# A two-level fast matrix product on one Trainium2 core: whole products in three places of the end groups, fewer range sums, and new hand-made orders at both ends

## The chip, the cores and the metric

The kernel runs on one core of one Trainium2 chip. Its time is the device time of one execution in microseconds (us); the number compared is the median over runs. Before the change it is 1456.9 us (three runs, 1456.58 to 1457.16).

## The reference

```python
B, S, D = 8, 2048, 2048
x = randn(B, S, D).float32;  w = randn(D, D).float32
cs = cumsum(x, axis=1)
diff = cs - concatenate([zeros, cs[:, :-1, :]], axis=1)   # this is x again
return matmul(diff, w).float32
```

The difference of a running sum is x itself, so the kernel computes C = x · w for 16384 rows, with inner and outer size 2048.

## The kernel before, in words

**Tiles and groups.** The 16384 rows are 128 tiles of 128 rows. The first four tiles (PLAIN, line 37) are multiplied plainly while the weights are still coming in (lines 178 to 358, matmuls at L264 and L299). The other 124 are done in 31 groups of four tiles (g, h, k, l), which `group` (line 566) writes down; `period[0]` counts the groups from 0 to 30.

**Two levels.** A group is a product of a 2x2 block matrix (rows g,h and k,l; two halves of the inner size) with a 2x2 block matrix of weights, done by the seven-product scheme of Strassen and Winograd: P1 to P7. P6 is done as a whole product, 2 x 16 matmuls (`whole_product`, L543). Each of the other six is itself 2x2 quarters. `Seven` does it with seven quarter products of four 128x512 matmuls each (`quarter`, L450) in place of eight. A group is thus 6 x 28 + 32 = 200 matmuls.

**What a Seven costs beside its matmuls.** `slot` (lines 476 to 505) records, for each product: four sums s1 to s4 of the x quarters on VectorE (128x512 f16); sums of weight quarters Q1, Q3, Q4 (128x2048 f16) that `Right.ask` (line 395) makes in one scratch area, `flow`, just before use, unless they have been made for good; one VectorE sum `middle` of two PSUM banks' contents; three ScalarE copies out of PSUM, `first`, `out2` and `out4`, on which later quarter products into the same bank wait; and one more sum, `last`, mostly on GpSimd. The sums of x between the outer products are S1 to S4 (128x1024 f16), applied in place to the x tiles. `keep` copies and `C..+P..` sums carry results out of PSUM into C tiles and add the products up, on ScalarE, VectorE and GpSimd.

**Weight quarters made for good.** For each right-hand block some sums are made once, by `Right.quarters` and `Right.make` (lines 379 to 394): Q3, Q2 and for some Q4. Q2 is written over t12, so t12 itself is gone from then on. For in_3 (used by P3) and in_7 (used by P7) these are six VectorE operations of 128x2048 f16 in group 0.

**Loads.** An x tile half is loaded by SyncE into one of three stages of F (`load`), cast to f16 by ScalarE (`narrow`), summed in magnitude by ScalarE for a range check (`weigh`; its throw-away output goes to the spare half of the same stage), and turned by a transposing DMA from SyncE's queue (`turn`). A stage is free for the next load only after both.

**The range sums of C.** `see` (line 507) makes ScalarE read a finished C tile (128x1024) and sum its magnitudes, with the throw-away output in the spare half of the stage that was loaded last. Before, all eight C tiles of group 1 are read so. `judge` (line 699) turns all checks into one flag (flag1 to flag9, a small matmul among them); the flag is read by every engine at the end (L1184), and a slow fallback (not taken here) hangs on it.

**The order.** Every operation is recorded with a label, and `emit` (line 104) sorts them by a number: group times 100000 plus the place of its label in the table `places` (line 733). An engine issues its operations in just this order, and waits in it for data. Groups 0, 1, 2, 28, 29 and 30 have a table of their own, all others share one (`None`). Each GpSimd operation also waits for the VectorE operation ahead of it in that order (`in_turn`).

Of the kernel before, what the change touches and what calls it, by code (L numbers as in the profile page):

```python
# [10 lines left out]
def kernel(  # L11
# [6 lines left out]
    nc = tc.nc  # L18
# [30 lines left out]
    const = ctx.enter_context(tc.tile_pool(name="const", bufs=1))  # L49
    Wall = const.tile([P, KH, 4 * NH], f32, name="W")  # L50
# [7 lines left out]
    seen_c = tiny[:, 8:16]  # L58
# [309 lines left out]
    class Right:  # L368
# [58 lines left out]
    in_3.quarters(early[3])  # L427
    in_7.quarters(late[0], late[1])
# [7 lines left out]
    for some, to in zip((in_3, in_5, in_1, in_2), late[3:]):  # L436
        some.make("Q4", "t21", "Q2", SUB, to)

# [23 lines left out]
    class Seven:  # L462
        def __init__(self, name, g, h, side, right, to, room, lent):
# [3 lines left out]
            self.right = right  # L467
            (self.g0, self.g1), (self.h0, self.h1) = to
# [6 lines left out]

        def slot(self, i):
            n = self.name
# [29 lines left out]
    def see(c, i):  # L507
        if period[0] == 1:
# [4 lines left out]
                lambda: nc.scalar.activation(other, c, ABS, accum_out=seen_c[:, i : i + 1]),  # L513
# [52 lines left out]
    def group(g, xy, zv):  # L566
        h, k, l = g + 1, g + 2, g + 3
# [3 lines left out]
        def ready(t, i):  # L571
            nonlocal ready_last
            ready_last = t, i
# [125 lines left out]
    def judge():  # L699
# [4 lines left out]
        dve("flag4", lambda: ins.tensor_scalar(flags[:, 8:16], seen_c, FINITE, None, ALU.is_le))  # L704
        dve("flag5", lambda: ins.tensor_reduce(flags[:, 1:2], flags[:, 8:16], AX.X, ALU.min))
# [36 lines left out]
            'first x.0.0': -710913, 'cast w.0.0': -708588, 'numbers turned': -640017,  # L742
            'eye': -620640, 'first x.0.1': -615478, 'first x.2.3': -611089,
# [517 lines left out]
```

## Time and profile before

| | |
|---|---|
| median of three runs | 1456.9 us |
| the profiled execution, its own time | 1456.21 us |
| its span from first to last instruction | 1454.3 us |
| mean granted TensorE clock | 0.998 |
| matmuls | 6543 |
| busy: TensorE, VectorE, ScalarE, GpSimd | 1424.5, 1302.5, 1046.1, 552.1 us |

In the profile, PE is TensorE (PEld its weight loads), DVE is VectorE, ACT is ScalarE, POOL is GpSimd and SP is SyncE, which issues all DMAs. Lines of the code are L126 (all sums, whatever engine), L129 (all ScalarE copies and casts), L163 (`weigh`), L513 (`see`), L450 and L543 (matmuls). Tiles are named without numbers: b is a PSUM bank, x the turned x tiles, F the stages, W the weights and their sums, arena everything else. Since one line covers many operations, an operation is found by its shape, its tiles and its position in the order.

### The profile page before, as it was taken

To read this page: it belongs to the slowest core of one execution; us is meant where nothing else is said; L and a number is where in the kernel's file an instruction comes from. 1 tells how busy PE (TensorE), PEld (TensorE's weight loads), DVE (VectorE), ACT (ScalarE), POOL (GpSimd) and SP (SyncE) were. 2 spreads that over 40 slices of the span, in tenths; PEclk is the share of its full clock that TensorE was granted. 3 is DMA by queue.
4 is the path that set the end of the run, shared out by engine and by line. 5 is a ranking of instruction groups with operands and counts; after the bars stand their busy time and mean duration, and the time that the engine had idled before them with its cause. 6 is when DMAs were issued, how large, how long until landed. Compare 5 with 4: busy or idle time off the path is not lost. (4 is left out here: it accounts for less than half of the span.)

```text
span 1454.3 us, 20618 instructions
## 1 busy us (share of the span) xinstructions
PE 1424.5 (98%) x6543; PEld 630.1 (43%) x6543; DVE 1302.5 (90%) x2107; ACT 1046.1 (72%) x1716; POOL 552.1 (38%) x376
## 2 busy tenths in 40 slices
PE   8999899999999999999999999999999999999997
PEld 3443334444444444444444444444444444444443
DVE  2799879999999999999999999999999999999997
ACT  5877867777777767777777777777777777776773
POOL 0014423444433444433444433444433444433444
PEclk9999999999999999999999999999999999999999
DMA  9998698888888898788888888898888898888883
GB/s 362 350 259 217 188 231 237 250 249 229 240 243 239 247 249 230 239 241 240 247 250 229 242 236 244 247 254 225 246 238 240 252 253 222 247 239 226 252 223 121
DMA packets 343792, 351.64 MB, mean 242 GB/s; under 512 B 270976, under 2 KB 270976, under 8 KB 343680
## 3 DMA queue, kind: packets, MB, share of 16 engines
q1 hardware_dynamic: 343680, 350.29, 84.3%
q8 instruction: 52, 0.85, 0.2%
q14 instruction: 60, 0.49, 0.1%
HBM read 150.99 MB, written 134.22 MB: 196 GB/s over the span
## 5 line engine op out<-in xcount | busy, mean ns | idle before, releaser
L126 POOL TENSOR_TENSOR arena<-arena 128x512 f32<-128x512 f32 x372 | 551.9, 1491 | 896.8 <-DVE arena L126 623.7
L129 ACT COPY arena<-b 128x512 f32<-128x512 f32 x729 | 407.2, 588 | 257.6 <-PE b L450 127.7
L450 PE MATMUL b<-W,x 128*128 128x512 f16 x2108 | 521.2, 379 | 2.1 <-DVE x L126 1.0
L450 PEld LDWEIGHTS <-x 128*128 128x128 f16 x3224 | 314.5, 98 | 396.4 <-issue 21.9
L126 DVE TENSOR_TENSOR arena<-W 128x2048 f16<-128x2048 f16 (+1 forms) x287 | 367.6, 1281 | 23.5 <-PE b L450 23.4
L450 PE MATMUL b<-W,arena 128*128 128x512 f16 x1364 | 344.0, 379 | 5.8 <-DVE arena L126 3.8
L450 PEld LDWEIGHTS <-arena 128*128 128x128 f16 x1984 | 189.1, 98 | 254.8 <-DVE arena L126 35.9
L129 ACT CAST F<-F 128x1024 f16<-128x1024 f32 x248 | 260.2, 1049 | 44.5 <-DMA F<-in_x_dram 40.6
L450 PE MATMUL b<-arena,x 128*128 128x512 f16 x1116 | 281.6, 379 | 4.4 <-ACT arena L129 4.4
L163 ACT ACTIVATE F<-F 128x1024 f16<-128x1024 f16 x248 | 263.1, 1062 | 1.1
L126 DVE TENSOR_TENSOR arena<-arena,b 128x512 f32<-128x512 f32 x372 | 247.7, 678 | 11.1 <-PE b L450 9.6
L543 PE MATMUL b<-W,x 128*128 128x512 f16 x992 | 250.1, 381 | 1.6 <-DVE x L126 1.6
L126 DVE TENSOR_TENSOR x<-x,x 128x1024 f16<-128x1024 f16 (+1 forms) x372 | 232.8, 633 | 6.2 <-DMA x<-F 3.8
L129 ACT COPY b<-b 128x512 f32<-128x512 f32 x186 | 107.3, 577 | 78.0 <-DVE arena L126 62.0
L450 PE MATMUL b<-arena 128*128 128x512 f16 x620 | 159.1, 379 | 2.3 <-DVE arena L126 2.1
L126 DVE TENSOR_TENSOR b<-b,arena 128x512 f32<-128x512 f32 x217 | 150.1, 692 | 11.4 <-ACT arena L129 11.0
L543 PEld LDWEIGHTS <-x 128*128 128x128 f16 x992 | 95.3, 98 | 122.3 <-DVE x L126 12.0
L126 DVE TENSOR_TENSOR arena<-b,arena 128x512 f32<-128x512 f32 x155 | 105.3, 681 | 18.5 <-PE b L450 17.0
L126 DVE TENSOR_TENSOR arena<-x,x 128x512 f16<-128x512 f16 x124 | 56.8, 458 | 31.9 <-PE b L450 31.7
L126 DVE TENSOR_TENSOR arena<-x 128x512 f16<-128x512 f16 x124 | 59.3, 479 | 1.2 <-PE b L450 0.2
L126 DVE TENSOR_TENSOR x<-x 128x512 f16<-128x512 f16 x124 | 56.6, 457 | 3.3 <-PE b L450 1.5
L126 DVE TENSOR_TENSOR arena<-arena,x 128x512 f16<-128x512 f16 x124 | 54.2, 437 | 2.6
(43 smaller groups left out, 301.4 us busy)
## 6 DMA issues: line engine op xcount, KB each, us to landing
F<-in_x_dram SPq DMA_DIRECT2D x248, 512.0 KB, 5.0
out_dram<-arena SPq DMA_DIRECT2D x240, 512.0 KB, 3.7
W<-in_w_dram SPq DMA_DIRECT2D x32, 512.0 KB, 9.0
out_dram<-arena SPq DMA_DIRECT2D x32, 256.0 KB, 3.4
W<-in_x_dram SPq DMA_DIRECT2D x16, 256.0 KB, 7.0
x<-F SPq DMA_TRANSPOSE x248, 3.2
```

Source lines behind the costliest of these rows:

```text
L126: record(label, engine, lambda: on.tensor_tensor(dst, p, q, op))
L129: record(label, "act", lambda: nc.scalar.copy(to, p))
L163: return nc.scalar.activation(other, data, ABS, accum_out=m)
L450: said = nc.tensor.matmul(to, a[:, ds(k * P, P)], b[:, k, :], start=(start and k == 0), stop=(k == 3), skip_group_check=True,)
L543: said = nc.tensor.matmul(to[n], half(t, 0)[:, k, :], T2[k][:, n, :], start=False, stop=(k == KH - 1), skip_group_check=True,)
```

## The change

Four things are changed.

1. `see` sums three C tiles in place of eight: C21 of rows l in group 29 (`see.3`), and C11 and C12 of rows h in group 30 (`see.1`, `see.5`). In group 1 there is none any more. The small checks read three columns in place of eight.
2. P3 and P7 in group 0, and P7 in group 30, are done as whole products: `slot_whole` records eight quarter products (w0 to w7) with no sums, no copies and no `last`. Each has 32 matmuls in place of 28. In group 30, t12 of in_7 is no longer there, so it is made again as t22 - Q3 in `flow`.
3. The weight sums of in_3 and in_7 (three each) are recorded in group 1 in place of group 0. In the new order the first of them stands early in group 0, three more amid the C12 sums of group 0, and two (in7 Q2 and Q4) in group 1.
4. The tables of places for groups 0, 1, 2, 28, 29 and 30 are new; the shared one is the same.

```diff
+    FROM3, FROM7 = 1, 1
+    LAST = (END - PLAIN) // 4 - 1
...
+                "t12": ("t22", "Q3", SUB),
...
-    in_3.quarters(early[3])
-    in_7.quarters(late[0], late[1])
...
-    for some, to in zip((in_3, in_5, in_1, in_2), late[3:]):
+    for some, to in zip((in_5, in_1, in_2), late[4:]):
...
+    def by_quarters():
+        if period[0] == FROM7:
+            in_7.quarters(late[0], late[1])
+        if period[0] == FROM3:
+            in_3.quarters(early[3])
+            in_3.make("Q4", "t21", "Q2", SUB, late[3])
...
+            self.whole = (name == "P3" and period[0] < FROM3) or (
+                name == "P7" and (period[0] < FROM7 or period[0] == LAST)
+            )
...
+        def slot_whole(self, i):
+            pairs = [
+                (to, a, b, start)
+                for to, p, q, c in (
+                    (self.g0, self.a11, self.a12, 1),
+                    (self.g1, self.a11, self.a12, 2),
+                    (self.h0, self.a21, self.a22, 1),
+                    (self.h1, self.a21, self.a22, 2),
+                )
+                for a, b, start in ((p, f"t1{c}", True), (q, f"t2{c}", False))
+            ]
+            for j in (0, 1) if i == 0 else (i + 1,):
+                to, a, b, start = pairs[j]
+                if b not in self.asked:
+                    self.asked[b] = self.right.ask(b)
+                quarter(f"{self.name}.w{j}", to, a, self.asked[b], start)
...
         def slot(self, i):
+            if self.whole:
+                return self.slot_whole(i)
...
     def see(c, i):
-        if period[0] == 1:
+        rows = {1: LAST, 5: LAST, 3: LAST - 1}
+        if i in rows and period[0] == rows[i]:
...
-                if s == "h" and i == 1:
+                if s == "h" and i == 1 and not P3.whole:
                     plus("P3.last", c[:, i, :], lz, "pool")
...
-                if s == "h" and i == 1:
+                if s == "h" and i == 1 and not P7.whole:
                     plus("P7.last", c[:, i, :], lx, "pool")
```

Parts of the new orders, as the tables give them, one engine each (the number ahead of the stroke is the group):

```
SyncE at the start:     x.0.2, x.0.1, w.0.2, x.0.3, x.0.0, w.0.0, x.1.0, x.1.3, x.1.1, w.0.1
  before:               w.0.1, x.0.3, w.0.0, x.0.0, x.0.1, x.2.3, x.1.1, x.0.2, x.2.2, x.1.0
SyncE, stores of the plain part: put out.0.0.0 is second, before it was sixth
TensorE, around 28/P1.6:  28/P1.6, 28/P2.2, 28/P6g.1.0     (before: 28/P1.6, 28/P6g.0.0)
TensorE, 29 to 30:      29/P4.2, 29/P7.6, 29/P7.5, 29/P4.4, 29/P4.3, 30/P1.0, 29/P4.6, 29/P4.5, 30/P2.0,
                        30/P1.3, 30/P1.2, 30/P1.1, 30/P2.3, 30/P1.4, 30/P1.5, 30/P1.6, 30/P2.2, 30/P2.1, 30/P2.4, 30/P2.5, 30/P5.0
ScalarE, 29 to 30:      30/P1.first, 29/narrow6.1, 29/weigh6.1, 29/see.3, 30/P2.first, 30/keep C11g.0, 30/P1.out2,
                        30/P1.out4, 29/narrow6.0, 30/keep C11g.1, 29/narrow7.1, 30/P2.out2, 29/narrow7.0
ScalarE, 1 to 2:        1/P4.out2, 1/weigh5.1, 1/P7.out4, 1/P4.out4, 1/narrow6.1, 1/weigh6.1, 2/P1.first,
                        1/narrow6.0, 2/P1.out2
TensorE, 1 to 2:        1/P4.2, 1/P4.3, 1/P7.4, 1/P4.4, 1/P7.6, 1/P7.5, 1/P4.6, 1/P4.5, 2/P1.0, 2/P1.1, 2/P1.2
ScalarE, 0 to 1:        0/weigh5.1, 0/weigh4.1, 0/P4.first, 0/P4.out2, 0/narrow6.1, 0/P4.out4, 0/narrow7.1,
                        1/P1.first, 0/narrow6.0, 1/P1.out2
TensorE at the end:     P7.w2, P4.2, P4.3, P4.4, P7.w3, P4.6, P4.5, flag8
VectorE at the end:     C21g+P7.1, vote, P4.s4, C21h+P4.0, C21g+P4.1, flag9
GpSimd at the end:      C22h+C21.0, C22h+C21.1, C22g+C21.0, P4.last, C22g+C21.1
  before:               C22h+C21.1, C22h+C21.0, C22g+C21.1, P4.last, ahead of them P7.last
```

More of the change, by code (lines that the diff above doesn't have):

```diff
@@ L57 @@
     seen_w = tiny[:, 0:1]
-    seen_c = tiny[:, 8:16]
+    seen_c = tiny[:, 8:11]
     flags = tiny[:, 16:32]
@@ L467, in __init__ @@
             self.right = right
+            self.whole = (name == "P3" and period[0] < FROM3) or (
+                name == "P7" and (period[0] < FROM7 or period[0] == LAST)
+            )
+            self.asked = {}
             (self.g0, self.g1), (self.h0, self.h1) = to
@@ L512, in see @@
                 "act",
-                lambda: nc.scalar.activation(other, c, ABS, accum_out=seen_c[:, i : i + 1]),
+                lambda: nc.scalar.activation(other, c, ABS, accum_out=seen_c[:, i // 2 : i // 2 + 1]),
             )
@@ L566, in group @@
     def group(g, xy, zv):
+        by_quarters()
         h, k, l = g + 1, g + 2, g + 3
@@ L572, in ready @@
             nonlocal ready_last
-            ready_last = t, i
+            if t < END:
+                ready_last = t, i
             load(t, i)
@@ L703, in judge @@
         dve("flag3", lambda: ins.tensor_reduce(flags[:, 0:1], fits, AX.XY, ALU.min))
[L704 to L705 removed]
+        dve("flag4", lambda: ins.tensor_scalar(flags[:, 8:11], seen_c, FINITE, None, ALU.is_le))
+        dve("flag5", lambda: ins.tensor_reduce(flags[:, 1:2], flags[:, 8:11], AX.X, ALU.min))
         dve(
@@ L734 @@
         0: {
[7 rows of a table removed]
-            'first x.0.0': -710913, 'cast w.0.0': -708588, 'numbers turned': -640017,
-            'eye': -620640, 'first x.0.1': -615478, 'first x.2.3': -611089,
[156 rows of a table removed]
-        },
[47 rows of a table removed]
-        },
[46 rows of a table removed]
[6 rows of a table added]
+            'first x.0.2': -1182588, 'ones': -1161467, 'numbers': -1151794,
+            'numbers turned': -1081308, 'first x.0.1': -1061770, 'w.0.2': -1026012,
[151 rows of a table added]
+        },
[48 rows of a table added]
+        },
[45 rows of a table added]
         },
         28: {
[44 rows of a table removed]
[45 rows of a table added]
         },
         29: {
[45 rows of a table removed]
[45 rows of a table added]
         },
         30: {
[43 rows of a table removed]
[42 rows of a table added]
         },
```

766 rows, old and new, of the table places are left out of this document.

## The prediction

> **What bounds the kernel now.** I read the page first, then busy time by stretches of one group's length, then the order of time where TensorE lost time.
>
> ```profile
> span 1454.3 us, 20618 instructions
> PE 1424.5 (98%) x6543; PEld 630.1 (43%) x6543; DVE 1302.5 (90%) x2107; ACT 1046.1 (72%) x1716; POOL 552.1 (38%) x376
> ...
> F<-in_x_dram SPq DMA_DIRECT2D x248, 512.0 KB, 5.0
> ...
> x<-F SPq DMA_TRANSPOSE x248, 3.2
> ```
>
> TensorE is the bound. An average of 98% leaves nothing to see of the ends, so the second view cuts the span; its columns are the length of the stretch, then busy time and count of PE, PEld, DVE, ACT and POOL, then the granted clock.
>
> ```profile
> 0.00:35.00 35.00, 28.53 (x155) 13.28 (x156) 10.00 (x22) 19.81 (x20) 0.20 (x4) 1.00 0.96 360
> ...
> 72.00:76.00 4.00, 2.68 (x13) 1.10 (x12) 4.00 (x6) 2.45 (x6) 0.00 (x0) 1.00 1.15 294
> 76.00:119.60 43.60, 41.82 (x190) 18.18 (x190) 42.13 (x61) 32.85 (x56) 10.48 (x7) 1.00 0.91 249
> 119.60:163.10 43.50, 40.05 (x181) 17.14 (x180) 38.95 (x62) 33.59 (x56) 13.91 (x10) 1.00 0.76 214
> 163.10:206.60 43.50, 38.51 (x166) 16.26 (x165) 35.68 (x56) 30.83 (x53) 12.16 (x9) 0.96 0.79 204
> ...
> 306.00:349.50 43.50, 43.50 (x202) 19.32 (x201) 40.05 (x66) 31.89 (x54) 17.78 (x13) 1.00 0.86 243
> 1305.10:1348.60 43.50, 42.47 (x197) 18.89 (x196) 40.70 (x66) 29.42 (x49) 17.90 (x12) 1.00 0.86 228
> 1360.00:1403.50 43.50, 42.85 (x197) 18.73 (x195) 40.28 (x66) 30.46 (x51) 16.59 (x12) 1.00 0.88 241
> 1403.50:1447.00 43.50, 41.69 (x189) 17.95 (x187) 40.41 (x70) 20.57 (x37) 19.62 (x14) 1.00 0.48 150
> ```
>
> A group in the middle (306 to 349.5) has TensorE busy throughout with VectorE at 40.05 of 43.50. So 200 matmuls take 43.5 us, 0.2175 each and 0.87 for a quarter product, and a VectorE load of 40 does no harm. The middle groups keep their order, so nothing is won there. Lost are 1.3 us at 72, 1.8, 3.5 and 5.0 in groups 0, 1 and 2, 1.0 in group 28, 0.7 and 1.8 in the last two. In group 0 VectorE is nearly full (42.13); in groups 1 and 2 it is not, and there a queue must be blocked. The order of time shows by what:
>
> ```profile
> 175.89 1.06 ACT L513 ACTIVATE F<-arena 128x1024 f16<-128x1024 f32 x1
> 176.86 0.19 ACT L513 ACTIVATION_READ_ACCUMULATOR F<-arena 128x1 f32 x1
> ...
> 183.61 1.04 ACT L129 CAST F<-F 128x1024 f16<-128x1024 f32 x1 [2.90 <-issue]
> ```
> ```profile
> 177.07 0.33 SPq L145 DMA_DIRECT2D F<-in_x_dram  x1
> ```
> ```profile
> 185.94 1.02 PE L450 MATMUL b<-arena,x 128*128 128x512 f16 x4 [2.34 <-ACT arena L129]
> 187.37 3.40 PE L543 MATMUL b<-W,x 128*128 128x512 f16 x8 [0.40 <-DVE x L126]
> ```
>
> The last range sum of group 1 ends at 177.05, and the load of tile 6, half 0, goes out at 177.07: the sum throws its output into the stage which that load fills. Its cast is next in ScalarE's queue and waits until 183.61; the copy P2.out4 behind it is what the quarter product at 185.94 waits for. Then eight matmuls take 3.40 us where 1.74 is the pace: the clock was halved, 1.66 us more. Groups 0 to 2 thus lose 1.8 + 3.5 + 5.0 + 1.7 = 11.9 us.
>
> **The change part by part.** *Whole products.* Twelve more matmuls at 0.2175: 1.7 us in group 0 and 0.9 in group 30, in full, since TensorE is the bound. What goes:
>
> ```profile
> L126 DVE TENSOR_TENSOR arena<-W 128x2048 f16<-128x2048 f16 x283 | 366.0, 1293 | 23.5 <-PE b L450 23.4
> ...
> L126 DVE TENSOR_TENSOR b<-b,arena 128x512 f32<-128x512 f32 x217 | 150.1, 692 | 11.4 <-ACT arena L129 11.0 <-PE b L450 0.3
> ...
> L126 DVE TENSOR_TENSOR arena<-x 128x512 f16<-128x512 f16 x124 | 59.3, 479 | 1.2 <-PE b L450 0.2
> ...
> L126 DVE TENSOR_TENSOR arena<-x,arena 128x512 f16<-128x512 f16 x124 | 53.4, 431 | 3.0 <-PE b L450 3.0
> ```
> ```profile
> L129 ACT COPY arena<-b 128x512 f32<-128x512 f32 x729 | 407.2, 588 | 257.6 <-PE b L450 127.7 <-POOL arena L126 76.7 <-DVE b L126 26.5
> ...
> L129 ACT CAST F<-F 128x1024 f16<-128x1024 f32 x248 | 260.2, 1049 | 44.5 <-DMA F<-in_x_dram 40.6 <-issue 2.9 <-ACT F L163 0.5
> ```
>
> In group 0, VectorE loses eight sums of 0.43 to 0.48 (3.6), two middles of 0.69 (1.4) and two Q1 of 1.29 (2.6), 7.6 us in all, and ScalarE six copies of 0.59, 3.5 us. Four of the six moved weight sums now stand in that stretch, three will. So VectorE falls from 42.13 to about 33.3 there: far under the 40 that does no harm. I keep 0.7 of the 1.8 lost. Group 1 gets two weight sums, 2.6 us: 38.95 becomes 41.5, between the 40.05 that costs nothing and the 42.13 that came with 1.8. I keep 2.0 of its 3.5.
>
> GpSimd works more in group 1 (13.91) than in group 0 (10.48), and VectorE is slower beside it:
>
> ```profile
> 171.88 1.67 DVE L126 TENSOR_TENSOR arena<-W 128x2048 f16<-128x2048 f16 x1
> ...
> 175.82 1.21 DVE L126 TENSOR_TENSOR arena<-W 128x2048 f16<-128x2048 f16 x1
> ```
> ```profile
> 164.73 7.74 POOL L126 TENSOR_TENSOR arena<-arena 128x512 f32<-128x512 f32 x5
> ```
>
> The same sum took 1.67 as GpSimd finished and 1.21 with it quiet. I leave the two at the mean of 1.29; beside GpSimd throughout they cost 0.8 more. The Trainium skill ("GPSIMD Engine Reference", 1. Specifications) says that GpSimd's way to SBUF is shared with VectorE, with contention for VectorE instructions with two SBUF inputs, which these are. By that rule alone the sum below would be 0.8 higher; the trace agrees with the direction.
>
> *Range sums.* Eight of 1.06 + 0.19, 10 us of ScalarE, leave group 1, and with them the hold on the load. Of the 5.0 + 1.7 of group 2 the rows above name 2.3 + 0.4 + 1.7; with the new order I keep 1.3. Groups 0 to 2 keep 0.7 + 2.0 + 1.3 = 4.0 of 11.9: -7.9 (bounds 0 and -11.9), and +1.7 for the matmuls.
>
> *Hand-over at 72 us.*
>
> ```profile
> 74.20 1.30 ACT L129 COPY arena<-b 128x512 f32<-128x512 f32 x2 [1.42 <-DMA out_dram<-arena]
> 75.40 0.59 ACT L129 COPY b<-b 128x512 f32<-128x512 f32 x1
> ```
> ```profile
> 76.05 1.02 PE L450 MATMUL b<-W,arena 128*128 128x512 f16 x4 [1.37 <-ACT b L129]
> ```
>
> The first ScalarE copy waits for a buffer whose store (put out.0.0.0) stood sixth among the stores and is now second; three plain products also stand ahead of P1.2. -1.1 (0 to -1.4).
>
> *Start.* The first turn needs two x pieces. In the old order 1.84 MB are asked for up to the second of them (256 KiB for a piece of x, 512 for one of w), in the new one 1.31 MB; at 360 GB/s (first row of the stretches) that is 1.5 us less. But until 35 us the weights come no faster, and TensorE had 6.5 us idle there. -0.4 (-1.6 to +2).
>
> *Group 28.*
>
> ```profile
> 1320.07 1.90 PE L543 MATMUL b<-W,x 128*128 128x512 f16 x8 [1.03 <-DVE x L126]
> ```
>
> A product that waits for nothing, P2.2 (0.87), now stands ahead of this one: -0.9 (0 to -1.0).
>
> *Groups 29 to 30.* The three range sums are 3.8 us on a ScalarE with room (20.57 of 43.50). But see.3 holds the load of tile 6, half 0, exactly as see.3 of group 1 did. I walk the new order from the start of 29/P4.2. TensorE: 18 quarter products until P2.4, 15.7 us. ScalarE: P1.first ends 0.7 after the sixth product, at 5.9; narrow6.1 (1.05) and weigh6.1 (as long as a range sum of the same shape, 1.06 + 0.19) bring 8.2, see.3 9.4. Load: issued then, 5.0 to land, 14.4 to 14.8. Then narrow6.0 (1.05), keep C11g.1 (0.59), narrow7.1 (1.05) and P2.out2 (0.59): 18.1. P2.4 waits for P2.out2, 2.4 us late in all; I add 0.3 for small waits. The turned tile (1.2 of issue, 3.2 to land) reaches S1g at 20, no later than the products ahead of P5.0. So 2.7 us are lost in place of 2.5 now (0.7 + 1.8), and 0.9 of matmuls come on top: +1.0 (-1.6, if the load lands in time, to +5).
>
> *The tail.*
>
> ```profile
> 1446.09 1.03 PE L450 MATMUL b<-W,x 128*128 128x512 f16 x4
> ```
> ```profile
> 1446.73 0.69 DVE L126 TENSOR_TENSOR arena<-arena,b 128x512 f32<-128x512 f32 x1 [0.54 <-POOL arena L126]
> 1447.95 0.69 DVE L126 TENSOR_TENSOR arena<-arena,b 128x512 f32<-128x512 f32 x1 [0.53 <-POOL arena L126]
> ```
> ```profile
> 1442.78 6.36 POOL L126 TENSOR_TENSOR arena<-arena 128x512 f32<-128x512 f32 x5 [0.42 <-DVE x L126]
> ```
> ```profile
> 1415.92 34.35 SPq L534 DMA_DIRECT2D out_dram<-arena  x15
> ```
>
> Five GpSimd sums in a row end at 1449.14, VectorE's last sums wait for them, and the last store is issued by 1450.27, 3.1 after the last matmul. In the new order P7.last is gone. From the end of P7.w3: C21g+P7.1 (0.69), then GpSimd's last sum (6.36 / 5 = 1.3), ready at 2.2; P4.s4 (0.43) lets P4.5 start 0.6 late and end at 2.4; C21g+P4.1 (0.69) and the store's issue bring 3.9, 1.5 after the last matmul: -1.6 (0 to -2).
>
> ```profile
> L1184 ACTq TENSOR_LOAD <-tiny x1: 1050/1050/1050, 1444.6 to 1444.6; - x1
> ```
> ```profile
> out_dram<-arena SPq DMA_DIRECT2D x32, 256.0 KB, 3.4
> ```
>
> The flag of the checks now comes behind VectorE's last sum, and every engine reads it, up to 1.05 us, where before it was read at 1444.6. That lies beside the last store's 3.4 us to land and costs nothing; it would cost 1.1 without that cover.
>
> Sum: -7.9 + 1.7 - 1.1 - 0.4 - 0.9 + 1.0 - 1.6 = -9.2. The profiled execution took 1456.2 (span 1454.3 and 1.9 around it), so 1447.0; the median is 0.7 above that execution: 1447.7.
>
> **The rivals.** *Hand-over, not VectorE.* If the idle time of groups 0 and 1 and at 72 comes from copies between banks and not from a full VectorE, it stays: 1.1 + 1.5 + 1.1 less is won, 1451.4. For it: the row at 76.05 names ScalarE. Against: VectorE is busy 42.13 of 43.60. Chance 0.17.
>
> *A blocked ScalarE queue.* What cost 2.3 + 0.4 + 1.7 = 4.4 at 183.61 happens at the boundaries of groups 0 to 1, 1 to 2 or 29 to 30: a cast of tile 6 again stands ahead of copies that TensorE needs. One such stall gives 1452.1 (0.12), two 1456.5 (0.07), three 1460.9 (0.07): from the third on the kernel is slower than before. For it: see.3 of group 29. Against: at the other two boundaries no range sum holds the load, and the cast stands some seven products (6.1 us) behind weigh5.1, which frees its stage, against 5.0 us to land. The Trainium skill ("TensorE: Matmul & The Clock Gate", Part 1) halves the clock after an idle window of about 3.4 us; by that rule a stall of 2.3 wouldn't, and one place would give 1450.4. The trace disagrees: it halved for 3.40 us after gaps of 2.34 and 0.40.
>
> **How the numbers follow.** The forecast has 0.57. A difference of 0.2%, 2.9 us, is about what a measurement here tells from no change. Faster are the forecast, the first rival and one stall, 0.86, less 0.04 that spill over: 0.82. Within 0.2%: two stalls and the spill, 0.11. Slower: 0.07. Downwards the idle time of groups 0 to 2 could go further, by 4.0, and the end by 2.6; upwards the range takes in the first rival and one stall with the start's +2: 1442 to 1455.
>
> **What would show it.** Right: groups 0 and 2 at 43 us or more of TensorE per 43.5, VectorE near 33 in group 0; no halved clock near 187; a load of tile 6 issued right after see.3 near 1395 and TensorE waiting 1 to 2 us after it; the last store issued under 2 us after the last matmul. Wrong: a stall over 2 us in groups 0 or 1, VectorE above 42 in group 1 with TensorE under 41, or TensorE starved in the first 35 us.

## The result, and the profile after

The changed kernel takes 1445.88 us (median of six runs, 1445.18 to 1446.83) against 1456.32 us of the kernel before, six runs beside it: a ratio of 0.993, 95% interval 0.9917 to 0.9942, 10.4 us. The forecast was 1447.7 in 1442 to 1455. The profiled execution took 1446.83, its span is 1445.0 where it was 1454.3.

The first lines of the page of after: TensorE has 12 matmuls more and is busy 0.6 us more in a span that is 9.3 us shorter.

```profile
span 1445.0 us, 20589 instructions
...
PE 1425.1 (99%) x6555; PEld 631.7 (44%) x6555; DVE 1289.3 (89%) x2090; ACT 1036.1 (72%) x1697; POOL 546.1 (38%) x373
```

Busy time by stretches, after; the columns are as in the prediction's table (length, then PE, PEld, DVE, ACT, POOL, then the granted clock):

```profile
0.00:35.00 35.00, 29.89 (x164) 14.28 (x165) 9.47 (x20) 19.98 (x20) 0.20 (x4) 0.95 0.96 352
35.00:72.00 37.00, 36.14 (x169) 16.27 (x167) 22.38 (x44) 31.31 (x41) 0.00 (x0) 1.00 1.07 356
72.00:76.00 4.00, 4.00 (x20) 1.83 (x19) 4.00 (x6) 3.53 (x7) 0.00 (x0) 1.00 1.03 376
76.00:119.60 43.60, 43.09 (x200) 19.20 (x197) 40.13 (x65) 31.64 (x53) 8.94 (x7) 1.00 0.90 253
119.60:163.10 43.50, 42.25 (x194) 18.73 (x193) 41.36 (x64) 30.47 (x52) 15.58 (x11) 1.00 0.81 214
163.10:206.60 43.50, 43.06 (x197) 18.96 (x196) 39.72 (x64) 31.11 (x52) 16.70 (x12) 1.00 0.94 240
206.60:250.10 43.50, 41.01 (x188) 18.11 (x187) 39.66 (x62) 30.68 (x51) 14.05 (x10) 1.00 0.86 239
...
1305.10:1348.60 43.50, 43.42 (x199) 18.98 (x198) 40.01 (x66) 31.82 (x53) 18.27 (x13) 1.00 0.82 228
```

Groups 0 to 2 now lose 0.5, 1.25 and 0.4 us, not 1.8, 3.5 and 5.0, and the halved clock of the third is gone. The 1.3 us at 72 are gone, but 0.9 are now lost between 35 and 72. And the stretch of group 3, which the prediction never looked at, loses 2.5. Both were full in the kernel before (0.0 and 0.2 lost):

```profile
35.00:72.00 37.00, 37.00 (x179) 17.04 (x178) 28.68 (x57) 32.34 (x42) 0.00 (x0) 1.00 1.06 352
...
206.60:250.10 43.50, 43.29 (x198) 18.83 (x197) 39.38 (x64) 31.38 (x52) 17.55 (x12) 1.00 0.87 241
```

The order of time of TensorE and then of VectorE shows the loss of group 3 (in brackets the idle time ahead of the instruction and what ended it):

```profile
212.21 1.04 PE L459 MATMUL b<-W,arena 128*128 128x512 f16 x4 [1.32 <-DVE arena L128]
...
224.95 1.02 PE L459 MATMUL b<-W,arena 128*128 128x512 f16 x4 [0.85 <-ACT arena L131]
```
```profile
209.44 1.27 DVE L128 TENSOR_TENSOR arena<-arena,b 128x512 f32<-128x512 f32 x2
210.63 1.52 DVE L128 TENSOR_TENSOR arena<-arena,x 128x512 f16<-128x512 f16 x1
```

3/P1.2 at 212.21 waits for the sum P1.s2 at 210.63. It stands behind two additions of group 2, and it takes 1.52 us where sums of its kind mostly take 0.43. A wait costs TensorE about 0.16 us more than the idle time of its row: a quarter product shows 1.03 us from its first start to its last end, but in a stream the next one starts after 0.87 (29/P4.2 at 1385.41, the next at 1386.27). Counted so, the idle 1.32 and 0.85 are the 1.5 and 1.0 of an expectation below.

The end has a load and a wait where and when the prediction named them. These are SyncE's, ScalarE's and TensorE's rows of after:

```profile
1395.02 0.98 SPq L147 DMA_DIRECT2D F<-in_x_dram  x2
```
```profile
1393.85 1.06 ACT L546 ACTIVATE F<-arena 128x1024 f16<-128x1024 f32 x1 [0.34 <-POOL arena L128]
...
1399.82 1.04 ACT L131 CAST F<-F 128x1024 f16<-128x1024 f32 x1 [0.66 <-DMA F<-in_x_dram]
```
```profile
1403.36 1.97 PE L459 MATMUL b<-W,arena 128*128 128x512 f16 x8 [0.52 <-DVE arena L128]
```

The sum see.3 ends at 1395.0, the load of tile 6 goes out at 1395.02, its cast starts at 1399.82, and 30/P2.4 starts at 1403.36, 17.95 us after 29/P4.2 (the prediction's walk had 18.1). But the row names VectorE as its releaser. The ScalarE copy P2.out2, which the walk had P2.4 wait for, had ended at 1402.78; the sum P2.s3 at 1402.87 ends 0.5 us later, in a row of VectorE's without a break:

```profile
1401.67 0.68 DVE L128 TENSOR_TENSOR arena<-arena,b 128x512 f32<-128x512 f32 x1
1402.27 0.69 DVE L128 TENSOR_TENSOR b<-b,arena 128x512 f32<-128x512 f32 x1
1402.87 0.42 DVE L128 TENSOR_TENSOR arena<-x,x 128x512 f16<-128x512 f16 x1
```

And the tail, all engines in order of time:

```profile
1429.67 11.42 SPq L567 DMA_DIRECT2D out_dram<-arena  x10
...
1434.45 1.23 DVE L739 TENSOR_SCALAR tiny<-tiny 128x3 f32<-128x3 f32 x1
...
1437.20 1.02 PE L459 MATMUL b<-arena,x 128*128 128x512 f16 x4 [0.50 <-ACT arena L131]
...
1438.90 1.04 PE L459 MATMUL b<-W,x 128*128 128x512 f16 x4 [0.67 <-DVE x L128]
...
1440.04 0.69 DVE L128 TENSOR_TENSOR arena<-arena,b 128x512 f32<-128x512 f32 x1 [0.60 <-PE b L757]
```

The last quarter product ends at 1439.94 and the last store is issued by 1441.09, 1.2 us later; before it was 3.1. The comparison at 1434.45 (flag4) takes 1.23 us, and in its wake P4.middle on VectorE, the copy P4.out4 on ScalarE and the quarter product P4.6 at 1437.20 come late.

**One measure for all runs.** Total times hide which end an edit moved, and the middle, the same in every kernel, differs by over 4 us from one profiled execution to another. So all kernels below are also cut at the starts of the first quarter product of groups 0, 4 and 28 and at the last instruction of an engine or of SyncE's stores, as the order of time has them (us):

| kernel | start of group 0 | 0 to 4 | 4 to 28 | 28 to last | ratio to before, 95% interval |
|---|---|---|---|---|---|
| before | 72.4 | 186.3 | 1046.4 | 145.2 | 1 |
| after | 71.1 | 179.0 | 1046.7 | 144.3 | 0.993 (0.9917 to 0.9942) |
| after, once more | 72.0 | 178.9 | 1049.2 | 144.4 | 0.9934 (0.9922 to 0.9947) |
| before, sums moved | 72.6 | 183.6 | 1046.6 | 146.8 | 0.9988 (0.9978 to 0.9997) |
| after, sums in group 1 | 70.4 | 183.3 | 1047.9 | 144.0 | 0.9976 (0.9967 to 0.9986) |
| new front, old end | 70.0 | 178.3 | 1047.6 | 145.9 | 0.9944 (0.9932 to 0.9956) |
| old front, new end | 73.3 | 183.0 | 1047.3 | 145.5 | 0.9968 (0.9956 to 0.9981) |
| old group 0 alone | 72.7 | 191.1 | 1048.0 | 144.8 | 1.0021 (1.0012 to 1.0029) |
| whole products, old order | 72.5 | 183.8 | 1049.4 | 144.9 | 0.9993 (0.9982 to 1.0003) |
| steady order in 2 and 28 | 71.6 | 183.2 | 1049.4 | 151.7 | 1.0020 (1.0011 to 1.0028) |
| tail reordered | 71.6 | 178.2 | 1046.8 | 144.8 | 0.9938 (0.9925 to 0.9951) |
| matmuls at the start | 71.5 | 178.4 | 1045.1 | 144.0 | 0.9914 (0.9901 to 0.9926) |
| the same, and hand-over 2 to 3 | 69.8 | 177.5 | 1047.9 | 144.4 | 0.9912 (0.9899 to 0.9926) |
| before, matmuls at the start | 73.0 | 184.6 | 1048.9 | 144.5 | 1.0017 (1.0007 to 1.0027) |

The cut at group 0 does not fall behind the same work in both orders. The new order has eight plain matmuls (1.7 us) behind the first quarter product of group 0 that the old one has ahead of it: 326 matmuls stand ahead of the cut, not 334, and 796 from 0 to 4, not 780 (the other eight are those of the whole products). So where a kernel with the new order of the start is set against one with the old (the old order have: before; sums moved; old front; old group 0; whole products, old order; and the last row), 1.7 us belong out of its 0 to 4 and into its start. Kernels with the same start can be compared as they stand.

### The profile page after: what moved, and what is told of

The parts are those of the page before. It is cut to its first block, busy times and chain, and to the rows that moved or that the text cites. A ratio compares the mean times of both kernels' runs of the same rounds, so it can differ in the third digit from the quotient of the medians.

```text
span 1445.0 us, 20589 instructions
## 1 busy us (share of the span) xinstructions
PE 1425.1 (99%) x6555; PEld 631.7 (44%) x6555; DVE 1289.3 (89%) x2090; ACT 1036.1 (72%) x1697; POOL 546.1 (38%) x373
## 5 line engine op out<-in xcount | busy, mean ns | idle before, releaser
L128 POOL TENSOR_TENSOR arena<-arena 128x512 f32<-128x512 f32 x369 | 545.9, 1488 | 893.7 <-DVE arena L128 498.6
L128 DVE TENSOR_TENSOR arena<-W 128x2048 f16<-128x2048 f16 (+1 forms) x284 | 360.4, 1269 | 22.5 <-PE b L459 21.5
L459 PE MATMUL b<-W,arena 128*128 128x512 f16 x1348 | 340.4, 379 | 4.0 <-DVE arena L128 2.5
L459 PEld LDWEIGHTS <-arena 128*128 128x128 f16 x1952 | 186.3, 98 | 247.9 <-DVE arena L128 32.7
L459 PE MATMUL b<-arena 128*128 128x512 f16 x604 | 155.0, 379 | 1.6 <-ACT arena L131 0.9
L266 PE MATMUL b<-W,arena 128*128 128x512 f16 x240 | 55.8, 387 | 1.5 <-ACT W L131 1.4
L128 DVE TENSOR_TENSOR x<-x 128x512 f16<-128x512 f16 x122 | 53.5, 439 | 1.8
```

Source lines behind the costliest of these rows:

```text
L128: record(label, engine, lambda: on.tensor_tensor(dst, p, q, op))
L266: said = nc.tensor.matmul(to[n], xP[:, r, ko, :], b[:, n, :], start=(ko == 0), stop=(ko == KO - 1))
L459: said = nc.tensor.matmul(to, a[:, ds(k * P, P)], b[:, k, :], start=(start and k == 0), stop=(k == 3), skip_group_check=True,)
```

## The experiments

The theory to be tested is the prediction's: the front gained 7.3 us since VectorE was relieved in group 0 and the sums left ScalarE in group 1; the end gained little since see.3 holds a load. The rivals: the front's gain is the sums' alone; or it is the new order's, and neither part gives it by itself.

**The sums moved, nothing else.**

```diff
 # the kernel before
-        if period[0] == 1:
+        rows = {1: LAST, 5: LAST, 3: LAST - 1}
+        if i in rows and period[0] == rows[i]:
 # tables: see.0 to see.7 out of group 1; see.3 behind 29/weigh6.0; see.1, see.5, flag4 to flag9 late in group 30
```

> The kernel before, in which only the sums of magnitudes are changed: the eight in group 1 are gone and three stand at the end (one in group 29, two in group 30), as in the changed kernel; the orders, the quarters in group 0 and the four quarters of P7 in the last group stay. Theory A (the eight sums held up ScalarE's copies, and with them TensorE, in groups 1 and 2): about 5 us faster than before, ratio 0.9965, with TensorE's busy time in 119.6 to 163.1 and 163.1 to 206.6 above 42.5 us each. Theory B (VectorE was the late one, and the sums lay in ScalarE's spare time): within 1.5 us of before, ratio 0.999 to 1.001, and the idle time of groups 1 and 2 stays.

Neither, nearer to theory B. From 0 to 4 it takes 183.6, 2.7 us less. The stretch of group 2:

```profile
163.10:206.60 43.50, 39.06 (x177) 16.87 (x176) 36.99 (x57) 28.04 (x47) 14.65 (x10) 1.00 0.81 215
```

The granted clock is 1.00 where it was 0.96, so the halved clock (1.7 us) went with the sums; 4.4 us of idle time remain, and 3.3 in group 1 (40.20 of 43.50). In this profile the old end pays 1.6 us for the three sums (146.8 in place of 145.2); in that of the new front with the old end it is 0.7 (145.9).

**The sums back in group 1.**

```diff
 # the changed kernel
-        rows = {1: LAST, 5: LAST, 3: LAST - 1}
-        if i in rows and period[0] == rows[i]:
+        if period[0] == 1:
+            # throw-away output: spare half of the stage weighed last at that point of the order
 # tables: see.0 to see.7 in group 1, none in 29 and 30
```

> The changed kernel with all eight sums back in group 1, each at the place beside its neighbours that it had before (where the new order has its block finished only later, right behind that), and none at the end. Theory A: about 4 us slower than the changed kernel, ratio to before 0.996, with the loss in groups 1 and 2, and 1 us of it given back at the end, where the sum of group 29 no longer holds a load. Theory B: within 1 us of the changed kernel, ratio 0.993 or less.

Theory A: 4.3 us from 0 to 4, and 6 to 7 by the ratios (0.9976 against 0.993 and 0.9934), as the profiled execution is the fastest of this kernel's nine. ScalarE at the hand-over from group 1 to 2, and what TensorE makes of it:

```profile
170.19 1.06 ACT L552 ACTIVATE F<-arena 128x1024 f16<-128x1024 f32 x1 [1.26 <-POOL arena L128]
...
171.38 1.06 ACT L552 ACTIVATE F<-arena 128x1024 f16<-128x1024 f32 x1
...
172.43 1.03 ACT L131 CAST F<-F 128x1024 f16<-128x1024 f32 x1
173.37 1.05 ACT L552 ACTIVATE F<-arena 128x1024 f16<-128x1024 f32 x1
...
174.42 0.57 ACT L131 COPY b<-b 128x512 f32<-128x512 f32 x1
```
```profile
175.04 1.86 PE L467 MATMUL b<-W,x 128*128 128x512 f16 x4 [3.58 <-ACT b L131]
```

The copy P2.first at 174.42 stands behind three sums (L552) and a cast, and 2/P2.3 waits 3.58 us for it; its four matmuls then take 1.86 at half clock. It is the prediction's second rival, a blocked ScalarE queue, brought on by hand.

The same run answers for the end, where it has no sum at all: 28 to last is 144.0 against 144.3 and 144.4. ScalarE's cast of tile 6 and TensorE's 30/P2.4:

```profile
1403.68 1.05 ACT L131 CAST F<-F 128x1024 f16<-128x1024 f32 x1
```
```profile
1407.97 1.32 PE L467 MATMUL b<-W,arena 128*128 128x512 f16 x5 [0.52 <-ACT F L131]
```

No sum holds the load, and the cast waits for no transfer. Yet 30/P2.4 starts 13.6 us after the start of group 30 (1394.4) with 0.52 us idle ahead of it, as in the changed kernel (1403.36 - 1389.7 = 13.6, 0.52). This row names a ScalarE cast, which happens to end at that moment; but VectorE's sum P2.s3 ends 0.05 us ahead of P2.4 here as in the changed kernel, and the copy P2.out2 has ended 0.9 us ahead:

```profile
1407.50 0.42 DVE L128 TENSOR_TENSOR arena<-x,x 128x512 f16<-128x512 f16 x1
```

So see.3 costs P2.4 nothing, and all three sums cost the end 0.3 to 0.4 us at most.

**The new front with the old end.**

```diff
 # the changed kernel
-            ... name == "P7" and (period[0] < FROM7 or period[0] == LAST)
+            ... name == "P7" and period[0] < FROM7
 # tables 28 to 30 as before, the three sums put in
```

> The changed kernel with the old orders of groups 28 to 30 (the three sums put into them at the places that the changed kernel gives them) and P7 in four quarters in the last group. What it loses against the changed kernel is the worth of the new end. The traces of the two kernels put the end at 2.1 us from the last matmul on and the stretch of groups 28 to 30 at between 0 and minus 1 us. Theory A (the new end is worth what the difference of the traces shows): 2 to 3 us slower than the changed kernel, ratio to before 0.9945 to 0.995. Theory B (the end is set by the last blocks' additions in any order): within 1 us of the changed kernel.

28 to last is 145.9, 1.6 us more than in the changed kernel, with four matmuls (0.9 us) fewer. The ratio, 0.9944, is 0.001 to 0.0014 above the two of the changed kernel, which is within their intervals. That is between the two theories; by the cut, the new end is worth some 1.6 us against an old end with the same three sums.

**The old front with the new end.**

```diff
 # the changed kernel
-    FROM3, FROM7 = 1, 1
+    FROM3, FROM7 = 0, 0
 # tables 0 to 2 as before, without the eight sums
```

> The changed kernel with the old orders of groups 0 to 2 and P3 and P7 in quarters in group 0 (eight matmuls fewer, four combinations for VectorE more), the eight sums left out of group 1 and three at the end as in the changed kernel. Theory A (the sums alone were the trouble of the front): 1 to 2 us slower than the changed kernel, ratio to before 0.994 to 0.9945. Theory B (the whole products and the new orders make the front's gain): 5 us slower, ratio 0.9965 or more.

Theory B: 0 to 4 takes 183.0, 4.0 us more than the changed kernel as cut and 5.7 at the same plain work, ratio 0.9968. Without sums the old front is as slow here as in the first run (183.6). So of the front's 9.0 us at the same plain work (7.3 as cut) the sums have 2.7 to 3.3 in the old order, and whole products and orders together the rest, 5.7 to 6.3.

**Whole products in the old order.** In this kernel and in the next, orders that were not made for each other are joined: some products read a block before its new content is there, so that part of C differs. Every instruction is there in its number and size, but a wait can be missing, so their times are a sign and no more.

```diff
 # the old front, new end, as above, but
+    FROM3, FROM7 = 1, 1
 # table 0: P3.w0 to w7, P7.w0 to w7 at the places of the quarters' slots; in3 and in7 makes in table 1
```

> The old orders of groups 0 to 2 without the eight sums, the new end, and in group 0 P3 and P7 as whole products at the places of their old quarters (the right-hand sides for the later quarters are made in the same stretch, as far as the places of the old order allow). So against the old front without its sums (183.1 us from the first quarter of group 0 to that of group 4) only the whole products are new: eight matmuls more, worth 1.7 us of TensorE, and the sums and intermediate additions of 14 quarters fewer on VectorE. Theory A (VectorE was the late one in group 0, and any order would profit): 180 to 181.5 us. Theory B (the whole products help only in an order made for them): 183 to 187 us.

Theory B, 183.8 us. The two stretches of groups 0 and 1:

```profile
76.00:119.60 43.60, 43.19 (x198) 19.18 (x198) 33.11 (x48) 30.10 (x52) 8.84 (x6) 1.00 0.90 243
119.60:163.10 43.50, 39.38 (x180) 17.07 (x178) 40.15 (x62) 30.25 (x50) 12.72 (x10) 1.00 0.76 216
```

In group 0 the prediction's sum holds to the tenth: VectorE falls to 33.11 (forecast 33.3), and TensorE fills up, 0.4 us idle in place of 1.8. But group 1 then loses 4.1 with VectorE at 40.15, the load that costs nothing in the middle. All four waits of group 1 end with a VectorE sum (1.70, 0.85, 1.00 and 0.48 us), the two longest here:

```profile
127.59 1.90 PE L459 MATMUL b<-W,arena 128*128 128x512 f16 x8 [1.70 <-DVE arena L128]
...
153.52 1.02 PE L459 MATMUL b<-W,x 128*128 128x512 f16 x4 [1.00 <-DVE b L128]
```

Groups 0 to 2 idle 8.3 us in place of the 9.7 of the old front without sums, and the eight matmuls more take 1.7: nothing is won.

**The old group 0 before the new groups 1 and 2.**

```diff
 # the changed kernel
-    FROM3, FROM7 = 1, 1
+    FROM3, FROM7 = 0, 0
 # table 0 as before; table 1 as after, fitted to the old table's times at its start, without the makes
```

> The changed kernel with the old order of group 0, P3 and P7 in quarters there (eight matmuls fewer), and the new orders in groups 1 and 2 (one load of group 1 put behind the turn that frees its place). Between the start of the first quarter of group 0 and the start of the first quarter of group 4 the kernel before took 186.3 us in its profile, the old front without its eight sums 183.6 and 183.1, the changed kernel 179.0. Theory A (the whole products and the order of group 0 carry what the sums do not): 182.5 to 183.5 us, ratio to before 0.996 to 0.997. Theory B (groups 1 and 2 gain by their own orders): 179.5 to 181 us, ratio 0.994 to 0.995.

Neither: 191.1 us, 12 more than the changed kernel (as cut) and 5 more than the kernel before. The stretches of groups 1 and 2 have TensorE at 37.68 us each. Here an order written for what one group leaves behind is worse than none of it when the group ahead is another.

**The steady order in groups 2 and 28.**

```diff
 # the changed kernel
-        2: {...}, 28: {...}     # both use the shared table
```

> The changed kernel with the order of groups 3 to 27 used in groups 2 and 28 as well, instead of their own orders. Theory A (TensorE's waits of 1.5 us before 3/P1.2 and 1.0 us before 3/P2.4 come of group 2's own order, whose tail leaves VectorE late): both waits shrink to under 0.4 us, but group 2 itself starts with what group 1 leaves and loses 1 us; the stretch from the first quarter of group 2 to that of group 4 is 1 to 2 us shorter than the 84.6 us of the changed kernel, and groups 28 to 29 are unchanged within 0.5 us. Theory B (group 1 leaves VectorE behind whatever the order of group 2): the waits move but the sum of the stretch stays within 0.5 us.

Neither. The waits at the hand-over from 2 to 3 do go: from the first quarter of group 3 to that of group 4 it is 43.5 us, not 46.3. But group 2 starts with a long wait. TensorE, then ScalarE:

```profile
171.58 1.86 PE L459 MATMUL b<-W,arena 128*128 128x512 f16 x4 [5.16 <-ACT b L131]
```
```profile
168.68 1.05 ACT L131 CAST F<-F 128x1024 f16<-128x1024 f32 x1 [1.98 <-DMA F<-in_x_dram]
...
170.95 0.58 ACT L131 COPY b<-b 128x512 f32<-128x512 f32 x1
```

0 to 4 is 183.2; at the end it is 7.4 us worse. The casts of tiles 6 and 7 wait for their loads and stand ahead of the copy P1.first at 170.95: a blocked ScalarE queue again, from the order alone. Group 2's own order pays 2.8 us at its end to save 7.0 from 0 to 3 (132.7 in place of 139.7).

**The additions of the hand-over put back.**

```diff
 # the changed kernel, with the matmuls at the start (below); table 2
-            'C21g+P4.0': 80055, 'C21h+P4.0': 84536,
+            'C21g+P4.0': 85040.2, 'C21h+P4.0': 85040.4,
```

> The changed kernel with the ten matmuls at the start of the run before, and in group 2 two additions for VectorE (C21g+P4.0, C21h+P4.0) put behind 3/in1.Q1, so that the sums and the side that TensorE's 3/P1.2 and 3/P1.1 wait for come 1.2 us earlier. Theory A (the idle 3.0 us of TensorE at the hand-over from group 2 to 3 are a matter of VectorE's order): the stretch from the first quarter of group 3 to that of group 4 is 45 to 45.8 us instead of 46.3, and the ratio to before 0.9905 to 0.991. Theory B (VectorE has that much work there in any order): the waits move, and the stretch stays within 0.3 us of 46.3.

Theory A: from group 3 to 4 it is 45.3 us. VectorE, then TensorE:

```profile
208.19 0.89 DVE L128 TENSOR_TENSOR arena<-arena,x 128x512 f16<-128x512 f16 x1
209.08 2.21 DVE L128 TENSOR_TENSOR arena<-W 128x2048 f16<-128x2048 f16 x1
211.21 1.87 DVE L128 TENSOR_TENSOR arena<-arena,b 128x512 f32<-128x512 f32 x3
```
```profile
209.14 1.04 PE L468 MATMUL b<-W,arena 128*128 128x512 f16 x4
...
213.81 1.90 PE L468 MATMUL b<-W,arena 128*128 128x512 f16 x8 [0.58 <-DVE arena L128]
```

The additions now stand behind the sum and the weight side; 3/P1.2 no longer idles 1.32. Of that 1.0 us is kept, though a part returns at 213.81: an addition put back is an addition that comes later. The time as a whole does not tell, 0.9912 beside the 0.9914 of the ten matmuls alone.

**The tail reordered.**

```diff
 # the changed kernel, table 30, VectorE
-  in4.Q4, flag4, flag5, P4.middle, C21h+P4.1, flag6, C21g+P4.0, C21g+P7.1, vote, P4.s4, C21h+P4.0, C21g+P4.1, flag9
+  in4.Q4, P4.middle, C21h+P4.1, C21g+P4.0, P4.s4, C21g+P7.1, flag4, flag5, flag6, vote, C21h+P4.0, C21g+P4.1, flag9
```

> The changed kernel with VectorE's last fourteen operations in another order: the three comparisons of the sums (flag4, flag5, flag6) stand behind the sum P4.s4 and the addition C21g+P7.1, not ahead of P4.middle, so that TensorE's last two quarters (P4.6 and P4.5) are not late behind them. In the changed kernel TensorE idles 0.66 us ahead of P4.6 and 0.83 ahead of P4.5. Theory A (these two idles are the comparisons' doing): the last matmul of P4 ends 1.2 us earlier from the start of group 30, and the kernel is 1.2 us faster than the changed one, ratio to before 0.992. Theory B (the last blocks' additions set the end and only change places): within 0.4 us of the changed kernel.

Theory B. VectorE, then TensorE:

```profile
1437.19 0.87 DVE L128 TENSOR_TENSOR x<-x 128x512 f16<-128x512 f16 x1
...
1438.58 0.15 DVE L739 TENSOR_SCALAR tiny<-tiny 128x3 f32<-128x3 f32 x1
...
1439.34 1.39 DVE L128 TENSOR_TENSOR arena<-arena,b 128x512 f32<-128x512 f32 x2
```
```profile
1438.12 1.04 PE L459 MATMUL b<-W,x 128*128 128x512 f16 x4 [0.89 <-DVE x L128]
```

P4.6 no longer waits, and the last quarter product ends 0.5 us earlier, counted from the start of group 30 (1.2 were expected). But the last two additions start at 1439.34 and end with 1440.7, as in the changed kernel (1440.04 + 0.69). The comparisons only changed places with the additions, and VectorE's row of both ends as late in either order.

**Matmuls into the idle start.** In ten of the fourteen profiles, of old and new orders alike, the clock is halved for one or two windows between 10 and 20 us, behind idle time of TensorE; in the first profile of the kernel before it is not.

```diff
 # the changed kernel
+        record(f"fill.{i}", "pe", lambda: nc.tensor.matmul(banks[6], zeros[:, :P], zeros, start=True, stop=True))
 # seven behind plain.0.0.0, three behind plain.0.1.0
```

> The changed kernel with ten matmuls more (128 by 512, into a bank not yet in use, results thrown away) at the start, seven after plain.0.0.0 and three after plain.0.1.0, where TensorE idles 1.7 and 0.7 us in the changed kernel's profile before a window of 3.413 us at half clock. Theory A (that idle time halves the clock): no window at half clock between 12 and 24 us, 1 to 1.7 us faster than the changed kernel, ratio to before 0.992. Theory B (the half clock comes of something else, or the first blocks of x set the start anyway): the window stays or the start of group 0 stays within 0.5 us of 71.1 us, and the ten matmuls cost up to 1 us where the transfers arrive early.

It is as fast as theory A has it (0.9914 for 0.992), but not by its reason. Three stretches of the start with the matmuls, and then those of the changed kernel run beside it later:

```profile
16.00:20.00 4.00, 4.00 (x21) 1.86 (x20) 0.70 (x2) 1.81 (x3) 0.00 (x0) 1.00 1.03 405
20.00:24.00 4.00, 3.13 (x27) 1.65 (x25) 0.69 (x1) 2.60 (x3) 0.00 (x0) 1.00 1.04 400
24.00:28.00 4.00, 2.54 (x18) 1.30 (x17) 0.69 (x1) 3.06 (x4) 0.00 (x0) 1.00 1.03 400
```
```profile
16.00:20.00 4.00, 3.69 (x11) 1.41 (x11) 0.70 (x2) 2.21 (x3) 0.00 (x0) 0.61 1.03 408
20.00:24.00 4.00, 4.00 (x27) 1.98 (x26) 0.69 (x1) 3.00 (x3) 0.00 (x0) 1.00 1.05 404
24.00:28.00 4.00, 3.81 (x30) 2.14 (x29) 0.69 (x1) 3.69 (x4) 0.00 (x0) 1.00 1.04 401
```

The clock is 1.00 in place of 0.61, and TensorE then idles 2.3 us in the next two stretches, at the same 400 GB/s of transfers. Group 0 starts at 71.5, no earlier than without (71.1 and 72.0). Where the 2 to 3 us come from by which its median lies under that of the changed kernel stays open (the two intervals overlap); its profile has them mostly in groups 4 to 28 (1045.1 against 1046.7 and 1049.2), where nothing was changed.

**The same for the kernel before.**

```diff
 # the kernel before
+        record(f"fill.{i}", "pe", lambda: nc.tensor.matmul(banks[0], zeros[:, :P], zeros, start=True, stop=True))
 # six behind the warm-up, seven behind turn x.0.0
```

> The kernel before with thirteen matmuls more at the start (128 by 512, thrown away): six behind the warm-up and seven behind turn x.0.0, where TensorE idles 1.7 to 2.2 and 1.4 us in its profile. Theory A (the half clock after that idle time is common to both kernels and comes in some executions of either): no window at half clock before 30 us, 1 to 1.7 us faster than before where it had one, ratio 0.999 to 0.9995. Theory B (the old order of the start does not suffer from it): within 0.3 us of before, or slower by up to 1 us where x arrives early.

Theory A falls: no halved clock in its profile before the end, and no gain (1.0017). The other profiles with the old order of the start say the same: group 0 starts at 72.4 and 73.0 with no halved window ahead of it, at 72.5 and 72.6 with one, at 72.7 and 73.3 with two. So no cost of the halved clock shows at the start. That the transfers set it is argued from their 400 GB/s in every case, not shown.

**The changed kernel once more.**

> The changed kernel itself, once more, as the measure for the runs beside it: ratio to before 0.9917 to 0.9942 as the first time.

0.9934, as the first time. Its profile shows two groups in the middle of 44.7 us among such of 43.5, as those of other kernels do; so 4 to 28 is no measure of an edit.

## Why the prediction was right, and where its steps were not

**The sum, -9.2.** From profile to profile the span is 9.3 us shorter: 8.6 up to group 4, 0.9 from group 28 on, and 0.3 longer between, where nothing was changed. So the forecast's -9.2 came out, but in part because errors cancel: the front was forecast 0.9 too small and the end 0.6 too large.

**The front, -7.3.** From 0 to 4 the table has 186.3 - 179.0 = 7.3, the sum of the front's terms (-7.9 + 1.7 - 1.1) to the tenth. That is luck of the cut: at the same plain work it is 9.0. Counted from the start of the span, group 4 begins 8.6 us earlier (250.1 for 258.7), where the terms with the start's -0.4 came to -7.7. Of the 8.6, 0.5 lie in the start and 0.5 at the hand-over; groups 0 to 3 have 7.6, or 9.3 without the matmuls of the whole products, where the prediction had 7.9. Most of this 1.4 is probably a term that it left out: it counted idle time alone, and each wait costs 0.16 more. In the kernel before twelve waits over 0.25 us stand in groups 0 to 2, in the changed kernel five in groups 0 to 3: an estimate of 7 x 0.16 = 1.1.

What is kept is not where it was looked for either. Groups 0 to 2 keep 2.2 us of idle time (0.5 + 1.25 + 0.4), not "0.7 + 2.0 + 1.3 = 4.0"; the 1.8 more is lost again, and 0.5 beside it, in the stretch of group 3, where the prediction looked for nothing, "the middle groups keep their order". The order is the same there, but what group 2 leaves behind is not: additions that VectorE has not done yet. The 1.0 us of the hand-over run shows that this is in part a matter of order. Which of the new orders, of group 0, 1 or 2, carries the 5.7 to 6.3 us that the sums do not stays open: the two runs that take them apart join orders that were not made for each other.

**Group 0 and VectorE.** The sum "VectorE falls from 42.13 to about 33.3" came out in the run of whole products in the old order (33.11, idle 0.4). In the changed kernel the row has 40.13, because the new order makes weight sums in this stretch that the old one made ahead of it (between 35 and 72 VectorE is busy 22.38 us, not 28.68). The prediction had put that at nothing; "VectorE near 33 in group 0" was a wrong sign to look for. And since TensorE loses 0.4 us at 33.11 and 0.5 at 40.13, the load itself did not decide. What went in both are the quarter products 0/P3.5 and 0/P7.4, whose waits for VectorE sums were 0.51 and 0.88 of the 1.8 us in the kernel before; a whole product has no such sums.

**Group 1.** "I keep 2.0 of its 3.5" was read from VectorE's load, between 40.05 and 42.13: it was 41.36 with 1.25 us lost, and at 40.15 another order lost 4.1. The load did not decide here either. But nor did copies, as the first rival ("hand-over, not VectorE") has it: of the 3.5 us in the kernel before, 1.90 and 0.47 end with a VectorE sum and 0.77 with a ScalarE copy, and in the run of whole products all four waits end with sums. The sums come late although VectorE has room in the stretch; that their place in the order does it is the likely reason, and is not shown by itself. In the changed kernel one long wait is left, 1.13 us ahead of 1/P3.0, and it ends with a ScalarE copy.

**At 72 us** the 1.3 went as forecast (1.1), but ahead of it the first products of group 0, now earlier in the order, idle 0.9 that were not there: the term was worth some 0.5.

**The range sums.** 2.7 to 3.3 us in the old order, the 1.7 of the halved clock among them; 4.3 in the new one. Of the rows that the prediction named, the 2.3 and the 1.7 went when the sums alone were taken away. The 0.4 did not: in that run the same product idles 1.18 us, and the 0.52 ahead of 2/P2.4 become 1.15.

**The start, -0.4.** Group 0 starts 1.3 us earlier here, but with 1.7 us of plain matmuls fewer ahead of it. At the same count of matmuls (326) the plain part ends at 70.1 in place of 70.6, 0.5 earlier. One profile cannot show so little: in the six profiles with the new start and no added matmuls, group 0 begins anywhere from 70.0 to 72.0.

**Group 28, -0.9.** 1.0 idle became 0.1 (43.42 of 43.50).

**Groups 29 to 30, +1.0.** This step failed in its reason. The walk gave the time of the main rows (load at 1395.02, P2.4 at 17.95 for 18.1), but "see.3 holds the load of tile 6" is not what P2.4 waits for: without any sum it waits as long. P2.4 starts 2.3 us later than 18 quarter products at their pace (15.7); the waits on the way, 0.35 at 30/P1.2, 0.34 at 30/P2.2 and 0.52 at P2.4 itself, all end with a VectorE sum, and from 1399.10 to 1405.6 VectorE works without a break. That the walk along ScalarE's queue came to the same time was luck.

**The tail, -1.6.** The last store is issued 1.2 us after the last matmul (forecast 1.5; before 3.1), P4.5 is 0.67 late (0.6). Not foreseen: flag4 took 1.23 us and made P4.6 late by 0.50. The end as a whole, from group 28 on, is 0.9 us shorter; the terms came to -1.5.

**The range.** Its lower end does not follow from its own terms: 1447.7 - 4.0 - 2.6 is 1441.1, not 1442.

**Contention.** The prediction took 0 and gave 0.8 us as the price by the Trainium skill ("GPSIMD Engine Reference", 1. Specifications): VectorE instructions with two SBUF inputs contend with GpSimd. The trace of after bears the rule out. The two weight sums of group 1 for which the price was meant took 1.22 us each, so there the 0 was right; but P1.s2 at 210.63, with GpSimd at work beside it, took 1.1 us longer, one of the two reasons why 3/P1.2 is late.

**A blocked ScalarE queue.** No such stall came in the changed kernel. That the mechanism is real is shown by two orders that have it: 3.58 us and 5.16 us of idle time with "ACT b" as releaser. The price of 4.4, halved clock included, is about right for the first (4.3 us from 0 to 4) and too low for the second, where two windows of halved clock follow and 0 to 3 is 7.0 us longer.

## What to carry to other kernels

Where several engines are near full, an order by hand can be worth more than the work that is left out, but only behind the state that it was made for: leaving the sums out gave 3 us, whole products in the old order nothing, and the whole products in an order of their own with the sums gone 9.0 at the same plain work. Before two orders are compared by a cut at one instruction, count the work ahead of it in both. Look one stage past the last one that is edited, since what is late there is given back there. And when a walk along one queue gives the right time for a wait, take the suspect away all the same: another queue may end at the same moment.

## What the runs showed of the hardware

**VectorE beside GpSimd, by form.** Told apart by their first 0.4 us, in the trace of after, with GpSimd quiet throughout or at work for 0.3 us or more: 128x512 sums with all operands in f16 take 0.43 us at most in 415 quiet cases, and 0.61 in the median, 1.52 at most, in 79 cases beside it. Sums of 128x2048 in f16 take 1.23 at most (171 cases) and 1.39 in the median, 1.70 at most (79). Sums of 128x512 in f32 take 0.70 at most in both (285 and 446); all of them have an operand in a PSUM bank, where the f16 ones read both from SBUF. Which one began first matters: 223 f16 sums of 128x512, in whose first 0.4 us a GpSimd sum began, took 0.55 at most. A comparison of three columns took 0.15 in the reordered tail with GpSimd quiet and 1.23 in the changed kernel beside GpSimd.

**The clock.** It is halved for 3.413 us at a time after much shorter gaps than that: in after from 15.716 on, behind gaps of 1.7 and 0.5 us. The Trainium skill ("TensorE: Matmul & The Clock Gate", Part 1) has it after an idle window of about 3.4 us; the length agrees, the whole idle window does not, as TensorE was busy 1.79 of 4 us between 12 and 16. Filled with matmuls, the same stretch kept its clock. The traces give a bound. Cut each of the fourteen into windows of 3.413 us from the first entry of its clock record: in all 26 windows at full clock that were followed by one at half clock, TensorE was busy for 0.423 of the window or less, and in all 5869 that were followed by one at full clock, for 0.429 or more. So the idle 1.90 us ahead of 1/P1.4 in the kernel before left the clock alone (busy for 0.46 of that window), and 2.34 with 0.40 behind it did not (0.37).
